# Solve operations of a hybrid decoder layer tied behind the large products, and a longer key chain

## The chip, the cores and the metric

One core of one Trainium2 chip runs the whole layer in one launch. The metric is device time in microseconds (us), the median of three runs.

## The reference

A decoder layer with two branches in parallel on 512 tokens of width 2048: sliding-window attention (32 query heads, 4 key heads of 64) and a gated delta rule (16 key heads, 32 value heads of 128, chunks of 64 tokens). Cut to what matters here:

```python
proj = h @ w_in                                    # all projections
d_qkv = causal_conv_silu(d_qkv, conv_w)
dk = jnp.repeat(l2_norm(dk), rep, axis=2)          # key norm
decay = jnp.exp(jnp.where(tril, g[..., :, None] - g[..., None, :], -jnp.inf))
L = jnp.where(strict, einsum('bhncd,bhnsd->bhncs', k_beta, k) * decay, 0.0)
t_inv = triangular_solve(eye + L, eye, lower=True, unit_diagonal=True)   # 64 x 64 per head and chunk
u = t_inv @ v_beta
w = t_inv @ (k_beta * jnp.exp(g)[..., None])
# then a scan over chunks with the state S, a norm, a gate, and the output products
```

## The kernel before

**Channel tiles.** Nearly all of TensorE's (PE's) work is `channel_tile`: one 128-channel slice of a projection for all 512 tokens, 16 contraction tiles, each as three products of split operands (`mm3`: L240 whi·hh, L241 whi·hl, L242 wlo·hh). So a tile is 48 large matmuls of 128x512. The weights come by DMA from SyncE's (SP's) queue into `raw` and are split into `whi` (ScalarE, ACT, L61) and `wlo` (VectorE, DVE, L62) half a tile at a time.

**Steps.** All other work is written as Python generators beside the tiles. After every second contraction tile (six large matmuls) `channel_tile` calls `pump()`, one step: generators in `live` count down the number that they yielded and continue at zero. The solve is in `slow`: it adds a budget of 0.36 a step and continues when it has saved up the number that it yielded. This is the order in which the program is written; a scheduler then lists each engine's instructions by this priority and by when its own model thinks that operands are ready, so an instruction written late can be issued early on an engine that the model sees idle. At run time each engine works through its list in order.

**Key stage** (`delta_keys`, about 155 to 545 us). Sixteen key heads g. For each: a channel tile, `conv` (ACT and DVE), a transpose `ptk` on PE (four matmuls), `sumsq` on ACT (junk, L686), `ss` and eleven small DVE operations on 128x4 for 1/sqrt (`rsqrt`: rky, rkt, L68 to L73), the scaled `k` on ACT (L653), its transpose `ptkT` on PE, `kT` (ACT), the Gram matrix `pkk` on PE (L668) and its product with the decay matrix E on DVE (L671), which DMA stores in `lt_d` and `lab_d`. E comes as a DMA broadcast of a row of `g_rows` (`decay_load`, L691), is masked on GpSimd (POOL, `decay_mask`, L698 and L699) and goes through exp on ACT (L663). Four buffers hold E, two for each head. Heads 4 to 7 follow each other tile by tile; from head 8 on a merge gate's tile (`mb`) stands between two keys. `ptk`, `ptkT` and `pkk` share two PSUM buffers.

**Solve** (`solve`, twice: b = 0 for the heads of keys 0 to 7, b = 1 for 8 to 15). When the keys are done, A (128 x 64 x 64) is loaded from `lt_d`, multiplied by -beta (L722), and inverted on DVE by 62 rounds, each a product into `atmp` (L729) and a sum into A (L735) of up to 992 elements. Then ACT copies four pieces to `ta_d` (L740), A is multiplied by beta (L745) and stored in `ts_d`. The second solve uses the same buffer.

**Attention** (`attention`, to about 1112 us): eight tiles for each of four groups n, beside them for each group the norm scales (`ssb`, `pss`), scores S, softmax (sm), their transposes pP copied to pT, and the product O. **Heads** (`delta_heads`, to about 2224 us): five tiles for each of 16 groups, beside them the query, value and gate chains and the scan (pp, r, pv, vn, vs, pd, S, po), with PE, DVE and ACT in turn. Groups 0 to 7 need the first solve, 8 to 15 the second. The output products follow.

Of the kernel before, what the change touches and what calls it, by code (L numbers as in the profile page):

```python
# [11 lines left out]
ALU = mybir.AluOpType  # L12
# [4 lines left out]
P = 128  # L17
# [8 lines left out]
HD = 64  # L26
# [19 lines left out]
class Layer:  # L46
# [190 lines left out]
    def mm3(self, ps, w, x, first, last):  # L237
        nc = self.nc
        (wh, wl), (xh, xl) = w, x
        nc.tensor.matmul(ps, lhsT=wh, rhs=xh, start=first, stop=False)  # L240
        nc.tensor.matmul(ps, lhsT=wh, rhs=xl, start=False, stop=False)  # L241
        nc.tensor.matmul(ps, lhsT=wl, rhs=xh, start=False, stop=last)  # L242

    def channel_tile(self, name, xh=None, xl=None):

# [391 lines left out]
    def keys(self, wk, g, ps):  # L637

        nc = self.nc
        y = wk.tile([P, T], F32, tag="y", name="y", bufs=3)  # L640
        yield from self.conv(wk, ps, 16 + g, y)
        E = [self.decay_load(wk, 2 * g + e) for e in range(2)]
        yield 2
        pt = self.ptp.tile([P, T], F32, tag="tp", name="ptk")
        self.transpose4(pt, lambda c: y[:, c * P : (c + 1) * P])
        ss = self.sumsq(wk, pt)
        yield 3
        nc.vector.tensor_scalar(out=ss, in0=ss, scalar1=EPS, scalar2=None, op0=ALU.add)
        rk = self.rsqrt(wk, ss, NTB, "rk")
        yield 2  # L650
        k = wk.tile([P, NTB, P], F32, tag="k", name="k")
        for c in range(NTB):
            nc.scalar.activation(k[:, c, :], pt[:, c * P : (c + 1) * P], AF.Copy, scale=rk[:, c : c + 1])  # L653
        for e in range(2):
            self.decay_mask(E[e], 2 * g + e)
        yield 3
        pt = self.ptp.tile([P, T], F32, tag="tp", name="ptkT")
        self.transpose4(pt, lambda c: k[:, c, :])
        nc.sync.dma_start(out=self.k_d[g], in_=k.rearrange("p c d -> p (c d)"))
        kT = wk.tile([P, T], F32, tag="kT", name="kT")  # L660
        nc.scalar.copy(out=kT, in_=pt)
        for e in range(2):
            nc.scalar.activation(E[e], E[e], AF.Exp)  # L663
        yield 2
        pk = self.ptp.tile([P, NTB, P], F32, tag="tp", name="pkk")
        for c in range(NTB):
            sl = slice(c * P, (c + 1) * P)
            nc.tensor.matmul(pk[:, c, :], lhsT=kT[:, sl], rhs=kT[:, sl], start=True, stop=True)  # L668
        nc.sync.dma_start(out=self.kT_d[g], in_=kT)
        for e in range(2):  # L670
            nc.vector.tensor_tensor(out=E[e], in0=pk, in1=E[e], op=ALU.mult)  # L671
        yield 2
        for e in range(2):
            h = 2 * g + e
            b, hl = h // 16, h % 16
            for k2 in range(2):
                s = slice(k2 * HD, (k2 + 1) * HD)
                nc.sync.dma_start(out=self.lt_d[b, k2, hl].rearrange("c j i -> j c i"), in_=E[e][s, :, s])
            nc.sync.dma_start(out=self.lab_d[h], in_=E[e][0:HD, :, HD:P])
        self.keys_done.append(g)  # L680
# [8 lines left out]
    def decay_load(self, wk, h):  # L689
        E = wk.tile([P, NTB, P], F32, tag="E", name="E", bufs=4)  # L690
        self.nc.sync.dma_start(out=E.rearrange("p c i -> p (c i)"), in_=self.g_rows[h].partition_broadcast(P))  # L691
        return E
# [10 lines left out]
    def solve(self, wk, b, eng):  # L703

        nc = self.nc
        while not all(g in self.keys_done for g in range(8 * b, 8 * b + 8)):
            yield 1.0
        A = wk.tile([P, HD, HD], F32, tag="A", name="A", bufs=1)
        bet = wk.tile([P, HD], F32, tag="bet", name="bet", bufs=1)
        for k2 in range(2):  # L710
            s = slice(k2 * HD, (k2 + 1) * HD)
            nc.sync.dma_start(
                out=A[s].rearrange("u j i -> u (j i)"), in_=self.lt_d[b, k2].rearrange("h c j i -> (h c) (j i)")
            )
            nc.sync.dma_start(
                out=bet[s],
                in_=self.b_rows.rearrange("h (c k i) -> k (h c) i", c=4, k=2)[k2, b * HD : (b + 1) * HD, :],
            )
        yield 8.0
        nb = wk.tile([P, HD], F32, tag="nbet", name="nbet", bufs=1)  # L720
        eng.tensor_scalar(out=nb, in0=bet, scalar1=-1.0, scalar2=None, op0=ALU.mult)
        eng.tensor_tensor(out=A, in0=A, in1=nb.unsqueeze(1).to_broadcast([P, HD, HD]), op=ALU.mult)  # L722
        eng.memset(A.rearrange("u j i -> u (j i)")[:, 0 : HD * HD : HD + 1], 1.0)
        for m in range(1, HD - 1):
            n = HD - 1 - m
            yield 0.2 + 0.0023 * m * n
            tmp = wk.tile([P, 1024], F32, tag="atmp", name="atmp", bufs=1)
            t = tmp[:, : m * n].rearrange("p (j i) -> p j i", j=m)
            eng.tensor_tensor(  # L729
                out=t,  # L730
                in0=A[:, m : m + 1, m + 1 :].to_broadcast([P, m, n]),
                in1=A[:, :m, m : m + 1].to_broadcast([P, m, n]),
                op=ALU.mult,
            )
            eng.tensor_tensor(out=A[:, :m, m + 1 :], in0=A[:, :m, m + 1 :], in1=t, op=ALU.add)  # L735
        for q in range(4):
            yield 1.5
            tmp = wk.tile([P, 1024], F32, tag="atmp", name="atmp", bufs=1)
            t = tmp.rearrange("p (i j) -> p i j", j=HD)[:HD]
            nc.scalar.copy(out=t, in_=A[:HD, :, q * 16 : (q + 1) * 16].rearrange("u j i -> u i j"))  # L740
            nc.sync.dma_start(
                out=self.ta_d[b].rearrange("h c i j -> (h c) (i j)")[:, q * 1024 : (q + 1) * 1024], in_=tmp[:HD]
            )
        yield 4.5
        eng.tensor_tensor(out=A, in0=A, in1=bet.unsqueeze(2).to_broadcast([P, HD, HD]), op=ALU.mult)  # L745
        for k2 in range(2):
            s = slice(k2 * HD, (k2 + 1) * HD)
            nc.sync.dma_start(
                out=self.ts_d[b, k2].rearrange("h c j i -> (h c) (j i)"), in_=A[s].rearrange("u j i -> u (j i)")
            )  # L750
# [765 lines left out]
```

## Time and profile before

| | |
|---|---|
| three runs | 2980.03, 2968.28, 2978.56 us; median 2978.56 |
| profiled execution | 2967.88 us, span 2966.1 us, mean granted clock 0.991 |
| busy, share of span | PE 97%, PEld 79%, DVE 60%, ACT 37%, POOL 7% |
| solve's rounds on DVE | L729: 124 operations, mean 883 ns; L735: 124, mean 894 ns; from 316.7 to 794.4 us |
| A times beta or -beta on DVE | L722 and L745: four operations of 4.42 us |
| solve's copies on ACT | L740: eight, median 2078 ns |

A stretch of a row of busy times gives each engine's busy us with the number of its instructions, then the share of full speed that PE's clock was granted, the DMA engines' busy share and GB/s. In rows in order of time the first number is the start, the second the duration, and the brackets give the idle time of that engine ahead of it and what ended it. Matmuls overlap, so their recorded durations (0.39 us for a large one) do not add up to a span.

### The profile page before, as it was taken

How to read it: one execution, taken by the hardware profiler on the slowest of the kernel's cores; microseconds unless marked ns; L12 is line 12 of the kernel's file. 1: busy time of each engine (PE TensorE's matmuls, PEld its weight loads, DVE VectorE, ACT ScalarE, POOL GpSimd, SP SyncE). 2: the span in 40 equal slices, each digit the busy share in tenths (PEclk: the TensorE clock that was granted, in tenths of full speed). 3: DMA queues.
4: the chain of work that ended last, by engine and by line, in shares of the span. 5: the costliest groups of instructions: out<-in, count | busy, mean ns of one | idle time of the engine just before them, and what ended most of it. 6: DMA issues, size and time to landing. Idle time of an engine off the chain costs nothing.

```text
span 2966.1 us, 38006 instructions
## 1 busy us (share of the span) xinstructions
PE 2876.7 (97%) x14524; PEld 2355.9 (79%) x14524; DVE 1775.4 (60%) x2903; ACT 1089.9 (37%) x2103; POOL 201.8 (7%) x188
## 2 busy tenths in 40 slices
PE   6899999999999999999999999999999999999999
PEld 5677777877878778888888888888887887888887
DVE  5766899699865544545454444454545555434666
ACT  3355333333543433333333333333333232222343
POOL 0012220010000000001100000000100000000000
PEclk8999999999999999999999999999999999999999
DMA  9855645632332233333333333334338998855684
GB/s 334 315 161 188 180 134 163 171 96 75 103 116 88 89 132 124 116 122 127 115 124 125 108 122 108 122 115 125 105 114 304 317 320 293 296 169 176 233 325 173
DMA packets 184871, 498.31 MB, mean 168 GB/s; under 512 B 75217, under 2 KB 77777, under 8 KB 147313
## 3 DMA queue, kind: packets, MB, share of 16 engines
q1 hardware_dynamic: 184690, 495.90, 50.1%
q8 instruction: 114, 1.87, 0.3%
q14 instruction: 67, 0.55, 0.1%
HBM read 415.26 MB, written 78.33 MB: 166 GB/s over the span
## 4 chain that ended last, share of the span: by engine, by line
PE 78%; DVE 11%; DMA 6%; ACT 2%; issue 2%; SPq 0%; POOL 0%; DVEq 0%; POOLq 0%; ACTq 0%
PE mm L240 21%; PE mm L241 20%; PE mm L242 20%; DVE wlo L62 2%; PE m L242 2%; PE m L241 2%; PE m L240 2%; DMA oraw<-o_d 2%; DVE A L735 2%; DVE atmp L729 2%; DVE wa L403 1%; DMA E<-g_rows 1%; DMA gw<-in_w_ada_gate 1%; PE po L901 1%; PE pv L882 1%
## 5 line engine op out<-in xcount | busy, mean ns | idle before, releaser
L240 PE MATMUL mm<-hh,whi 128*128 128x512 f32 x2784 | 1134.4, 407 | 3.6 <-ACT mth L263 3.6
L242 PE MATMUL mm<-hh,wlo 128*128 128x512 f32 x2784 | 1093.3, 393 | 0.0
L241 PE MATMUL mm<-hl,whi 128*128 128x512 f32 x2784 | 1091.0, 392 | 0.0
L62 DVE TENSOR_TENSOR wlo<-raw,whi 128x1024 fp32r<-128x1024 f32 (+1 forms) x484 | 590.2, 1221 | 483.7 <-ACT whi L61 460.5
L61 ACT CAST whi<-raw 128x1024 fp32r<-128x1024 f32 (+1 forms) x484 | 504.8, 1044 | 938.6 <-PE mm L241 829.9
L242 PEld LDWEIGHTS mm<-hh,wlo 128*128 128x128 f32 x2784 | 524.8, 189 | 114.2 <-issue 0.7
L240 PEld LDWEIGHTS mm<-hh,whi 128*128 128x128 f32 x2784 | 525.9, 189 | 112.5 <-issue 8.3
L241 PEld LDWEIGHTS mm<-hl,whi 128*128 128x128 f32 x2784 | 526.4, 189 | 99.6 <-issue 0.8
L240 PE MATMUL mm<-oh,whi 128*128 128x512 f32 x512 | 202.5, 397 | 6.9 <-ACT oh L61 6.9
L241 PE MATMUL mm<-ol,whi 128*128 128x512 f32 x512 | 201.6, 394 | 0.6 <-DVE ol L62 0.6
L242 PE MATMUL mm<-oh,wlo 128*128 128x512 f32 x512 | 201.0, 393 | 0.0
L240 PEld LDWEIGHTS mm<-oh,whi 128*128 128x128 f32 x512 | 97.0, 190 | 29.5 <-ACT oh L61 8.6
L241 PEld LDWEIGHTS mm<-ol,whi 128*128 128x128 f32 x512 | 97.2, 190 | 23.0 <-DVE ol L62 2.1
L242 PEld LDWEIGHTS mm<-oh,wlo 128*128 128x128 f32 x512 | 97.3, 190 | 20.4
L735 DVE TENSOR_TENSOR A<-A,atmp 128x62 f32<-128x62 f32 (+30 forms) x124 | 110.8, 894 | 2.0
L729 DVE TENSOR_TENSOR atmp<-A 128x62 f32<-128x62 f32 (+30 forms) x124 | 109.5, 883 | 1.6
L829 POOL TENSOR_TENSOR qe<-qe,yq 128x512 f32<-128x512 f32 x32 | 46.7, 1479 | 921.9 <-DMA qe<-eg_rows 921.9
L698 POOL TENSOR_TENSOR E<-E,neg_g 128x512 f32<-128x512 f32 x64 | 75.0, 1173 | 412.2 <-DMA E<-g_rows 356.9
L875 DVE SCALAR_TENSOR_TENSOR r<-pp,neg_eg,vt 128x128 f32<-128x128 f32 x96 | 29.3, 346 | 92.4 <-PE pp L872 90.5
L1220 ACT ACTIVATE sm<-sm,mx,rs 128x256 f32<-128x256 f32 (+1 forms) x128 | 71.8, 562 | 5.0 <-DVE mx L1215 5.0
L566 DVE SCALAR_TENSOR_TENSOR yv<-mm,convh,yv 128x511 f32<-128x511 f32 (+2 forms) x96 | 71.4, 744 | 1.7
L403 DVE SCALAR_TENSOR_TENSOR wa<-wa,silu_cb 128x2048 f32<-128x2048 f32 x24 | 54.8, 2283 | 6.5 <-DMA silu_cb<-silu_d 6.5
(337 smaller groups left out, 3025.9 us busy)
## 6 DMA issues: line engine op xcount, KB each, us to landing
raw<-in_w_ch SPq DMA_DIRECT2D x158, 1024.0 KB
wa<-in_w_ada_ss SPq DMA_DIRECT2D x32, 1024.0 KB
raw<-in_w_od SPq DMA_DIRECT2D x32, 1024.0 KB
E<-g_rows SPq DMA_DIRECT2D x64, 256.0 KB
q<-in_w_out SPq DMA_DIRECT2D x32, 512.0 KB
gw<-in_w_ada_gate SPq DMA_DIRECT2D x16, 1024.0 KB
f_d<-q SPq DMA_DIRECT2D x32, 512.0 KB
raw<-in_w_os SPq DMA_DIRECT2D x16, 1024.0 KB
```

What stands on the lines that cost most here:

```text
L61: self.nc.scalar.copy(out=hi, in_=src)
L62: self.nc.vector.tensor_tensor(out=lo, in0=src, in1=hi.bitcast(F32), op=ALU.subtract)
L240: nc.tensor.matmul(ps, lhsT=wh, rhs=xh, start=first, stop=False)
L241: nc.tensor.matmul(ps, lhsT=wh, rhs=xl, start=False, stop=False)
L242: nc.tensor.matmul(ps, lhsT=wl, rhs=xh, start=False, stop=last)
L403: nc.vector.scalar_tensor_tensor(out=wa, in0=wa, scalar=1.0, in1=scb, op0=ALU.mult, op1=ALU.mult, accum_out=t[:, j : j + 1])
L566: nc.vector.scalar_tensor_tensor(out=y[:, s:], in0=ps[:, : T - s], scalar=w[:, j : j + 1], in1=y[:, s:], op0=ALU.mult, op1=ALU.add)
L698: nc.gpsimd.tensor_tensor(out=E, in0=E, in1=ng, op=ALU.add)
L729: eng.tensor_tensor(out=t, in0=A[:, m : m + 1, m + 1 :].to_broadcast([P, m, n]), in1=A[:, :m, m : m + 1].to_broadcast([P, m, n]), op=ALU.mult,
L735: eng.tensor_tensor(out=A[:, :m, m + 1 :], in0=A[:, :m, m + 1 :], in1=t, op=ALU.add)
L829: nc.gpsimd.tensor_tensor(out=qf, in0=qf, in1=q, op=ALU.mult)
L1220: nc.scalar.activation(t, t, AF.Exp, scale=r[:, h : h + 1], bias=mx[:, h : h + 1], accum_out=den[:, h : h + 1])
```

## The change

Four edits, all in the order of work; no instruction is added or taken away.

1. `mm3` remembers its last matmul, and `behind` gives an instruction an edge for the scheduler: it is listed after that matmul. The edge carries no semaphore. All DVE operations of the solve but the memset get it, so each is listed after the large product that was written last before it.
2. Each solve round, one step of product and sum before, is two steps of half the length, with the sum in the second.
3. In the key chain the pause between 1/sqrt and k goes from 2 steps to 4, and that between k and ptkT from 3 to 4. ptkT is written 3+4+4 = 11 steps (66 large matmuls) behind ptk, where it was 3+2+3 = 8 (48).
4. The two loads of decay rows move from two steps ahead of ptk to three steps behind it.

```diff
+        self.last_mm = nc.tensor.matmul(ps, lhsT=wl, rhs=xh, start=False, stop=last)
+    def behind(self, ins):
+        self.tc.add_manual_dep(
+            ins.ins, self.last_mm.ins.name, mybir.DependencyInfo(mybir.DependencyClass.NoSync, mybir.DependencyReason.DATA),
+            reason="pace",
+        )
...
         yield from self.conv(wk, ps, 16 + g, y)
-        E = [self.decay_load(wk, 2 * g + e) for e in range(2)]
         yield 2
         pt = self.ptp.tile([P, T], F32, tag="tp", name="ptk")
...
         yield 3
+        E = [self.decay_load(wk, 2 * g + e) for e in range(2)]
         nc.vector.tensor_scalar(out=ss, in0=ss, scalar1=EPS, scalar2=None, op0=ALU.add)
         rk = self.rsqrt(wk, ss, NTB, "rk")
-        yield 2
+        yield 4
...
             self.decay_mask(E[e], 2 * g + e)
-        yield 3
+        yield 4
...
         for m in range(1, HD - 1):
             n = HD - 1 - m
-            yield 0.2 + 0.0023 * m * n
+            yield 0.1 + 0.00115 * m * n
...
-            eng.tensor_tensor(
...
+            self.behind(
+                eng.tensor_tensor(
...
-            eng.tensor_tensor(out=A[:, :m, m + 1 :], in0=A[:, :m, m + 1 :], in1=t, op=ALU.add)
+            yield 0.1 + 0.00115 * m * n
+            self.behind(eng.tensor_tensor(out=A[:, :m, m + 1 :], in0=A[:, :m, m + 1 :], in1=t, op=ALU.add))
```

The edges reach the multiplications of A by -beta and by beta in the same way.

The order that results is compared at three places, all on DVE. Lines of the changed kernel are 7 to 10 higher (L648 is L655, L729 and L735 of the solve are L737 and L745, L722 is L729). First, key chain 13 in the key stage, from ss on; A and atmp are the solve's, rky and rkt the chain's. Before:

```order
L648 TENSOR_SCALAR ss<-ss 128x4
L735 TENSOR_TENSOR A<-A,atmp 128x33x30
L68 TENSOR_SCALAR rky<-ss 128x4
L62 TENSOR_TENSOR wlo<-raw,whi 128x1024
L71 SCALAR_TENSOR_TENSOR rkt<-rky 128x4
L729 TENSOR_TENSOR atmp<-A 128x986
L72 TENSOR_TENSOR rkt<-rkt,ss 128x4
L735 TENSOR_TENSOR A<-A,atmp 128x34x29
L73 SCALAR_TENSOR_TENSOR rky<-rkt,rky 128x4
L729 TENSOR_TENSOR atmp<-A 128x980
L71 SCALAR_TENSOR_TENSOR rkt<-rky 128x4
L62 TENSOR_TENSOR wlo<-raw,whi 128x1024
```

Now:

```order
L655 TENSOR_SCALAR ss<-ss 128x4
L68 TENSOR_SCALAR rky<-ss 128x4
L71 SCALAR_TENSOR_TENSOR rkt<-rky 128x4
L72 TENSOR_TENSOR rkt<-rkt,ss 128x4
L73 SCALAR_TENSOR_TENSOR rky<-rkt,rky 128x4
L71 SCALAR_TENSOR_TENSOR rkt<-rky 128x4
L62 TENSOR_TENSOR wlo<-raw,whi 128x1024
L72 TENSOR_TENSOR rkt<-rkt,ss 128x4
L73 SCALAR_TENSOR_TENSOR rky<-rkt,rky 128x4
L737 TENSOR_TENSOR atmp<-A 128x752
L71 SCALAR_TENSOR_TENSOR rkt<-rky 128x4
L72 TENSOR_TENSOR rkt<-rkt,ss 128x4
```

Between ss and the chain's last rky stood eight solve operations and two wlo; now one of each stands there. The solve has also come less far (752 elements on the way up, where it was at 986 on the way down).

Second, attention, where the changed kernel has the second solve's first multiplication (A by -beta, L729) and the softmax's copies pT of group 2; the kernel before has no solve operation between the two copies there.

```order
L1238 TENSOR_SCALAR sm<-sm,den 128x256 x8
L62 TENSOR_TENSOR wlo<-raw,whi 128x1024 x2
L728 TENSOR_SCALAR nbet<-bet 128x64
L1250 COPY pT<-pP 128x512
L729 TENSOR_TENSOR A<-A,nbet 128x4096
L1064 TENSOR_TENSOR partner_4384<-partner_4384,sin 128x512
L730 MEMSET A 128x64
L1065 TENSOR_TENSOR aq<-aq,partner_4384 128x512
L737 TENSOR_TENSOR atmp<-A 128x62
L1250 COPY pT<-pP 128x512
```

The multiplication of 4096 elements and one round's product now stand ahead of the second copy.

Third, the heads, in the tiles of group 2, where the scan's S and r stand between the query's convolution (yq). Before:

```order
L912 SCALAR_TENSOR_TENSOR S<-S,egl,pd 128x128 x2
L62 TENSOR_TENSOR wlo<-raw,whi 128x1024
L566 SCALAR_TENSOR_TENSOR yq<-mm,convh,yq 128x511
L566 SCALAR_TENSOR_TENSOR yq<-mm,convh,yq 128x510
L566 SCALAR_TENSOR_TENSOR yq<-mm,convh,yq 128x509
L875 SCALAR_TENSOR_TENSOR r<-pp,neg_eg,vt 128x128 x2
L573 SCALAR_TENSOR_TENSOR yq<-th,yq 128x512
L62 TENSOR_TENSOR wlo<-raw,whi 128x1024
```

Now:

```order
L922 SCALAR_TENSOR_TENSOR S<-S,egl,pd 128x128 x2
L62 TENSOR_TENSOR wlo<-raw,whi 128x1024
L573 SCALAR_TENSOR_TENSOR yq<-mm,convh,yq 128x511
L737 TENSOR_TENSOR atmp<-A 128x950
L573 SCALAR_TENSOR_TENSOR yq<-mm,convh,yq 128x510
L885 SCALAR_TENSOR_TENSOR r<-pp,neg_eg,vt 128x128 x2
L573 SCALAR_TENSOR_TENSOR yq<-mm,convh,yq 128x509
L580 SCALAR_TENSOR_TENSOR yq<-th,yq 128x512
L745 TENSOR_TENSOR A<-A,atmp 128x38x25
L62 TENSOR_TENSOR wlo<-raw,whi 128x1024
```

A product of the second solve has come between the convolution's parts ahead of r, and its sum behind them. In the whole head stage 74 such operations have come, the last of them in group 5; before there were none. On PE only ptkT and pkk, and some of the attention's pP and O, stand at another point between the large products.

More of the change, by code (lines that the diff above doesn't have):

```diff
@@ L241, in mm3 @@
         nc.tensor.matmul(ps, lhsT=wh, rhs=xl, start=False, stop=False)
-        nc.tensor.matmul(ps, lhsT=wl, rhs=xh, start=False, stop=last)
+        self.last_mm = nc.tensor.matmul(ps, lhsT=wl, rhs=xh, start=False, stop=last)
[4 more added lines that the diff above has]
+        )
     def channel_tile(self, name, xh=None, xl=None):
@@ L720, in solve @@
         nb = wk.tile([P, HD], F32, tag="nbet", name="nbet", bufs=1)
-        eng.tensor_scalar(out=nb, in0=bet, scalar1=-1.0, scalar2=None, op0=ALU.mult)
-        eng.tensor_tensor(out=A, in0=A, in1=nb.unsqueeze(1).to_broadcast([P, HD, HD]), op=ALU.mult)
+        self.behind(eng.tensor_scalar(out=nb, in0=bet, scalar1=-1.0, scalar2=None, op0=ALU.mult))
+        self.behind(eng.tensor_tensor(out=A, in0=A, in1=nb.unsqueeze(1).to_broadcast([P, HD, HD]), op=ALU.mult))
         eng.memset(A.rearrange("u j i -> u (j i)")[:, 0 : HD * HD : HD + 1], 1.0)
@@ L725, in solve @@
             n = HD - 1 - m
-            yield 0.2 + 0.0023 * m * n
+            yield 0.1 + 0.00115 * m * n
             tmp = wk.tile([P, 1024], F32, tag="atmp", name="atmp", bufs=1)
             t = tmp[:, : m * n].rearrange("p (j i) -> p j i", j=m)
[L729 to L733, printed above, removed]
-            )
-            eng.tensor_tensor(out=A[:, :m, m + 1 :], in0=A[:, :m, m + 1 :], in1=t, op=ALU.add)
+            self.behind(
+                eng.tensor_tensor(
+                    out=t,
+                    in0=A[:, m : m + 1, m + 1 :].to_broadcast([P, m, n]),
+                    in1=A[:, :m, m : m + 1].to_broadcast([P, m, n]),
+                    op=ALU.mult,
+                )
+            )
+            yield 0.1 + 0.00115 * m * n
+            self.behind(eng.tensor_tensor(out=A[:, :m, m + 1 :], in0=A[:, :m, m + 1 :], in1=t, op=ALU.add))
         for q in range(4):
@@ L744, in solve @@
         yield 4.5
-        eng.tensor_tensor(out=A, in0=A, in1=bet.unsqueeze(2).to_broadcast([P, HD, HD]), op=ALU.mult)
+        self.behind(eng.tensor_tensor(out=A, in0=A, in1=bet.unsqueeze(2).to_broadcast([P, HD, HD]), op=ALU.mult))
         for k2 in range(2):
```

## Prediction

> **What bounds the kernel now.** I read the page first, then busy time in stretches cut at the borders of the channel tiles, then the order of time around the gaps on TensorE (PE).
>
> ```profile
> span 2966.1 us, 38006 instructions
> PE 2876.7 (97%) x14524; PEld 2355.9 (79%) x14524; DVE 1775.4 (60%) x2903; ACT 1089.9 (37%) x2103; POOL 201.8 (7%) x188
> ```
>
> PE is busy for 97% of the span: the kernel ends when PE has issued its products. An edit to VectorE's (DVE's) order can gain only where PE waits for DVE, at most some 90 us. The next view has one row for each pair of channel tiles in the key stage: width, busy time of PE, PEld, DVE, ACT, POOL, granted clock, DMA share, GB/s. Each pair holds 96 large products and about one key chain.
>
> ```profile
> 257.47:288.15 30.68, 27.05 (x129) 22.47 (x128) 17.20 (x38) 14.20 (x36) 8.59 (x10) 0.94 0.59 182
> 288.15:312.70 24.55, 24.55 (x121) 20.60 (x120) 12.65 (x24) 10.62 (x26) 2.09 (x3) 1.00 0.77 211
> 312.70:340.51 27.81, 25.92 (x113) 20.88 (x112) 26.12 (x45) 9.95 (x23) 5.37 (x5) 0.94 0.61 191
> 340.51:370.85 30.34, 25.45 (x113) 20.78 (x112) 28.73 (x39) 11.41 (x25) 11.47 (x9) 0.94 0.44 144
> 370.85:398.52 27.67, 25.55 (x113) 20.80 (x112) 25.77 (x36) 9.94 (x23) 4.32 (x4) 0.94 0.35 110
> 398.52:426.36 27.84, 25.22 (x113) 20.58 (x113) 26.00 (x34) 10.05 (x23) 6.23 (x4) 0.94 0.43 139
> 426.36:454.18 27.82, 25.32 (x113) 20.67 (x113) 26.36 (x35) 10.04 (x23) 6.33 (x4) 0.94 0.45 145
> 454.18:479.97 25.79, 23.96 (x113) 19.56 (x113) 25.59 (x36) 10.07 (x23) 7.11 (x6) 1.00 0.45 143
> ```
>
> The pair at 288.15 runs undisturbed: 24.55 us, PE never idle, clock 1.00. From 312.70 on DVE is busy for 26 to 29 us of each pair, more than PE needs for one: in this stage DVE is the bound. The difference is the solve, whose instructions alone are these (DVE, ACT, then clock and DMA):
>
> ```profile
> 288.15:312.70 24.55, 0.62 (x1) 0.00 (x0) 1.00 0.77 211
> 426.36:454.18 27.82, 15.22 (x14) 0.00 (x0) 0.94 0.45 145
> ```
>
> How this reaches PE, for key chain 13 (DVE, ACT and PE rows in order of time):
>
> ```profile
> 426.90 0.16 DVE L648 TENSOR_SCALAR ss<-ss 128x4 f32<-128x4 f32 x1
> 432.94 1.01 DVE L71 SCALAR_TENSOR_TENSOR rkt<-rky 128x4 f32<-128x4 f32 x1
> 437.53 1.16 DVE L729 TENSOR_TENSOR atmp<-A 128x972 f32<-128x972 f32 x1
> 439.12 0.39 PE L242 MATMUL mm<-hh,wlo 128*128 128x512 f32 x1
> 441.39 0.15 DVE L73 SCALAR_TENSOR_TENSOR rky<-rkt,rky 128x4 f32<-128x4 f32 x1
> 441.58 1.15 ACT L653 ACTIVATE k<-ptk,rky 128x128 f32<-128x128 f32 x4 [0.21 <-DVE rky L73]
> 442.00 0.47 PE L274 MATMUL ptkT<-ident,k 128*128 128x128 f32 x1 [2.50 <-ACT k L653]
> 442.13 0.77 PE L240 MATMUL mm<-hh,whi 128*128 128x512 f32 x1
> ```
>
> Eleven small operations on 128x4, 0.15 us each when nothing disturbs them, take from 426.90 to 441.54, since solve operations stand between them. ACT scales k only then, and PE, in order, stands at ptkT for 2.50 us. The large product behind it takes 0.77 instead of 0.39 us: the clock has dropped.
>
> **The change, part by part.** It is summed against the profiled execution's own time, 2967.88 us (span 2966.1).
>
> *Key stage.* PE's idle time is width minus busy: 3.63, 0, 1.89, 4.89, 2.12, 2.62, 2.50 and 1.83, together 19.5 us. Six of the rows have clock 0.94; their widths sum to 172.2 us, and 6% of it is 10.3 us. So 29.8 us can be had here.
>
> With the edges, six solve operations stand between one chain's ss and the next one's, where there were 12 to 14; at 15.22/14 = 1.09 us each that takes DVE from 26.4 to about 26.4 - 15.2 + 6.5 = 17.7 us in a pair that needs 24.55. In chain 13 itself, one solve operation and one wlo (1.2 us) remain between ss and the last rky, where there were eight and two: at 1.1 to 1.2 us each some 9.4 us fewer, against the 2.50 us that PE waited. Three more steps between ss and ptkT add room: a step is 24.55/16 = 1.53 us, so 4.6 us for chains whose ptkT stood 48 large products behind ptk and now stands 66 behind; chains 11 to 14 stood at 62 to 67 already and gain by the shorter DVE queue. I leave 3 us, between 0 and 12 (three stalls like the one at 426.36: 2.50 + 1.7 each), for the chain that now meets the 4.42 us multiplication of A at its head. Gain 27.
>
> *Decay rows five steps later.* The stall in the row at 257.47 came before any solve operation. Its chain:
>
> ```profile
> 263.53 1.05 POOL L698 TENSOR_TENSOR E<-E,neg_g 128x512 f32<-128x512 f32 x1 [4.67 <-DMA E<-g_rows]
> 264.65 1.57 POOL L699 TENSOR_SCALAR_AFFINE_SELECT E<-E 128x512 f32<-128x512 f32 x1
> 266.26 0.63 ACT L663 ACTIVATE E<-E 128x512 f32<-128x512 f32 x1 [4.70 <-POOL E L699]
> 271.30 1.14 ACT L653 ACTIVATE k<-ptk,rky 128x128 f32<-128x128 f32 x4 [2.95 <-DVE rky L73]
> 257.71 5.69 DMA E<-g_rows
> 367.74 4.89 DMA E<-g_rows
> ```
>
> ACT stood 4.70 us for the mask on POOL, which waited for the rows, and with ACT the th that DVE's queue needed. The last two rows, from the chain of waits, give 4.9 to 5.7 us from a load's issue to its use. The load now comes three steps behind ptk and its product E with pkk 13 steps behind ptk; ten steps are 15.3 us, and 5.7 for the load, 2 x (1.05 + 1.57) on POOL and 2 x 0.63 on ACT make 12.2. It fits with 3.1 us to spare, and the loads ask for their buffers later, so SP stands less for the stores of chain g-2. Cost nothing, cover 3.1 us; if it is gone, the E exponentials hold ACT and kT is late next. The gain on this stall is in the 27.
>
> *Attention.* The four groups do equal work; each row is half a group:
>
> ```profile
> 615.37:671.32 55.95, 51.49 (x269) 40.86 (x269) 54.70 (x85) 17.06 (x34) 2.02 (x1) 0.97 0.26 80
> 671.32:729.67 58.35, 54.83 (x281) 42.77 (x281) 58.11 (x87) 23.47 (x52) 5.55 (x3) 1.00 0.21 73
> 729.67:789.24 59.57, 59.46 (x373) 47.16 (x373) 58.31 (x114) 24.18 (x55) 1.28 (x1) 1.00 0.29 98
> 789.24:846.16 56.92, 54.41 (x289) 43.52 (x289) 41.88 (x75) 32.30 (x58) 4.06 (x3) 1.00 0.51 143
> 903.57:957.72 54.15, 54.15 (x289) 43.52 (x289) 35.44 (x65) 24.40 (x54) 3.94 (x3) 1.00 0.27 90
> 957.72:1015.12 57.40, 57.40 (x365) 45.84 (x365) 31.79 (x75) 22.96 (x53) 1.29 (x1) 1.00 0.26 86
> 625.89 0.91 PE L1170 MATMUL pss<-ident,ssb 128*128 128x128 f32 x4 [4.46 <-DVE ssb L1166]
> 817.16 4.42 DVE L745 TENSOR_TENSOR A<-A,bet 128x4096 f32<-128x4096 f32 x1 [2.72 <-ACT atmp L740]
> 822.24 1.75 PE L1247 MATMUL O<-pT,vtok_a 128*64 128x128 f32 x28 [2.50 <-DVE pT L1240]
> ```
>
> Against the last group, without a solve, the rows lose 58.35 - 54.15 = 4.20, 59.57 - 57.40 = 2.17 and 56.92 - 54.15 = 2.77 us; the row at 615.37 loses 4.46 idle and 3% of clock, 1.7. Together 15.3 us. The solves now run through all of attention at half that density. New: the 4.42 us product of A and -beta stands ahead of one of two pT copies, as the product with beta did at 817.16, where PE lost 2.5 us. I leave 5 of the 15.3 (one such stall with clock, 4.2, and crumbs); bounds 0 and 15.3. Gain 10.
>
> *Heads.* Seventy-four solve operations, all in the second solve, move into the first six head groups, some 75 us of DVE work. There DVE has room (first row), and the scan's r, ready at 1259.50, is used by pv at 1261.46:
>
> ```profile
> 1240.80:1644.64 403.84, 403.84 (x2138) 336.15 (x2137) 201.00 (x378) 150.68 (x337) 36.29 (x36) 1.00 0.37 119
> 1258.89 0.61 DVE L875 SCALAR_TENSOR_TENSOR r<-pp,neg_eg,vt 128x128 f32<-128x128 f32 x2
> 1261.46 0.60 PE L882 MATMUL pv<-r,tt 128*128 128x128 f32 x4
> ```
>
> The 1.96 us cover one operation of 1.2 us. The 4.42 us product with beta stands once ahead of the E product with pqk. I take 2 us of loss, between 0 and 10 (1.6 us in each of six groups). PE's written order is otherwise unchanged here.
>
> *The edges and the halved steps* add no instruction, and no wait on PE: in the built program the solve operations wait for DVE and DMA alone, as before. Cost nothing; nothing is queued behind a new wait.
>
> Sum: 27 + 10 - 2 = 35 us, 2967.88 - 35 = 2933. The profiled execution equals the lowest of the runs shown (2968.28); the others are 2978.56 and 2980.03. Two of four lie near 2968 and two near 2979, so I add half the distance, 5.5: **2938 us**.
>
> A rule to weigh: the six rows with clock 0.94 followed PE gaps of 1.89 to 4.89 us. The Trainium skill, "TensorE: Matmul & The Clock Gate", section "What's actually happening", lets the clock fall only after an idle window of about 3.4 us. By that rule only three of the gaps above (3.63, 4.89, 4.46) would have cost clock, and the gain would be 4 x 1.7 = 6.8 us smaller; the rows show the drop after 1.89 to 2.62 us too, so the trace disagrees and the sum stands by the rows.
>
> **Rivals.**
>
> *The heads give it back (slower).* If DVE has no slack at the scan's hand-overs, each solve operation there delays PE by its length. For it: r, vs, S and vn alternate between PE and DVE in every group. Against: 1.96 us of slack, and the attention row at 671.32, with DVE busy 58.11 of 58.35 us, lost only 4.20. In full it costs 75 us: 2967.9 - 37 + 75 = 3006. It decides from 37/75, half of the work exposed.
>
> *The edges don't touch what is late.* Then the late masks on POOL hold the chains, as at 263.53 without any solve, and loading later does not help: the key stage keeps its 29.8. Against: the undisturbed pair at 288.15 had the same masks. Only attention gains: 2967.9 - 10 + 5.5 = 2963.
>
> *Spread but not relieved.* The key stage gains its 27, attention none, as the solves stay in it longer, and the heads lose 5: 2967.9 - 22 + 5.5 = 2951.
>
> **How the numbers follow.** Forecast 0.70, spread 0.17, edges miss 0.09, heads 0.04. Low end: all of 29.8 + 15.3 from 2967.9, 2922. High end: between the second-best case and the third, 2960; about 0.13 is left above it. A measurement here tells 0.5% from no change, 14.9 us: faster means under 2963.7. All of the forecast and of the spread case are faster, 0.87; the 2963 case counts as same, 0.09; slower 0.04.
>
> **What would show it.** Right: rows of the key stage with PE idle under 1 us each and clock 1.00, DVE near 18 us a pair; solve operations from about 340 us to about 1500 us; head groups still 67 us. Wrong: ptkT waiting for k by over 2 us in more than two chains, pv or pu waiting for DVE in the first six groups, or ACT standing for POOL ahead of k.

## The result and the profile after

The changed kernel takes 2941.45 us (median of 4 runs, 2938.28 to 2947.28); beside it the kernel before took 2973.42 us (2966.49 to 2980.03). The ratio is 0.9894, 95% interval 0.9874 to 0.9915: faster by about 1.1%. The profiled execution took 2939.34 us.

```profile
span 2937.5 us, 37979 instructions
PE 2865.5 (98%) x14524; PEld 2350.7 (80%) x14524; DVE 1764.5 (60%) x2903; ACT 1088.3 (37%) x2103; POOL 208.6 (7%) x188
```

PE is still the bound; 28.6 us of span went, 11.2 of them out of its busy time, in which stretches of slower clock count in full. The pairs of key tiles, cut and laid out as in the prediction (width; busy PE, PEld, DVE, ACT, POOL; clock; DMA share; GB/s):

```profile
255.49:281.04 25.55, 25.55 (x130) 21.38 (x128) 17.35 (x38) 15.33 (x42) 8.15 (x8) 1.00 0.61 198
281.04:306.12 25.08, 25.08 (x126) 20.99 (x124) 12.26 (x23) 11.38 (x24) 6.75 (x6) 1.00 0.90 240
306.12:329.77 23.65, 23.65 (x113) 19.70 (x112) 14.02 (x23) 9.43 (x21) 1.69 (x2) 1.00 0.64 184
329.77:354.46 24.69, 23.91 (x114) 19.62 (x112) 20.16 (x39) 10.98 (x24) 9.20 (x8) 1.00 0.61 194
...
425.42:449.07 23.65, 23.65 (x113) 19.70 (x112) 16.34 (x27) 10.05 (x22) 5.33 (x5) 1.00 0.51 151
```

PE is idle in one of eight pairs (0.78 us), and the clock is whole. DVE has about 16 us of work in a pair of 23.65, where it had 26; only the pair with the solve's first, short rounds has 20. The solve alone in the last pair (DVE, ACT), and key chain 13:

```profile
425.42:449.07 23.65, 6.29 (x6) 0.00 (x0) 1.00 0.51 151
```

```profile
425.82 0.17 DVE L655 TENSOR_SCALAR ss<-ss 128x4 f32<-128x4 f32 x1 [0.18 <-ACT junk L693]
429.27 0.16 DVE L73 SCALAR_TENSOR_TENSOR rky<-rkt,rky 128x4 f32<-128x4 f32 x1
429.46 1.14 ACT L660 ACTIVATE k<-ptk,rky 128x128 f32<-128x128 f32 x4 [2.24 <-DVE rky L73]
439.05 0.60 PE L281 MATMUL ptkT<-ident,k 128*128 128x128 f32 x4
```

The chain takes 3.6 us instead of 14.6, and k lies ready 8.5 us before ptkT.

By stages, the kernel before first: key stage (from the second mb tile to the first key tile of attention), attention, and head groups 0 to 5.

```profile
166.42:547.33 380.91, 360.40 (x1669) 296.10 (x1668) 291.52 (x477) 164.59 (x356) 73.75 (x66) 0.97 0.54 169
570.99:1112.69 541.70, 528.94 (x2948) 422.53 (x2946) 404.36 (x721) 219.43 (x458) 31.21 (x26) 1.00 0.31 100
1112.69:1510.07 397.38, 397.38 (x2088) 330.29 (x2089) 192.17 (x349) 145.24 (x316) 37.64 (x36) 1.00 0.38 121
```

```profile
166.05:515.77 349.72, 348.88 (x1669) 289.73 (x1668) 223.41 (x408) 156.11 (x350) 69.30 (x66) 1.00 0.57 176
539.43:1069.19 529.76, 525.62 (x2948) 420.99 (x2946) 393.40 (x712) 218.32 (x458) 35.49 (x26) 1.00 0.34 106
1069.19:1484.77 415.58, 404.40 (x2089) 334.76 (x2089) 259.32 (x425) 152.30 (x320) 44.17 (x36) 0.98 0.40 124
```

So the key stage gained 31.2 us and attention 11.9, and the heads lost 18.2. The remaining 4 us lie in stages that the change doesn't touch (the start, and the wait for transfers behind the heads). The heads' loss, group by group (1 to 5):

```profile
1132.07:1202.21 70.14, 67.45 (x359) 55.95 (x358) 46.71 (x75) 25.02 (x57) 7.77 (x6) 1.00 0.35 114
1202.21:1273.86 71.65, 69.07 (x360) 57.22 (x358) 45.76 (x75) 25.02 (x57) 8.09 (x6) 0.98 0.35 111
1273.86:1345.75 71.89, 69.00 (x360) 57.18 (x358) 46.59 (x78) 25.03 (x57) 7.70 (x6) 0.98 0.35 111
1345.75:1417.46 71.71, 68.95 (x360) 57.14 (x358) 45.16 (x88) 28.85 (x59) 7.49 (x6) 0.98 0.38 116
1417.46:1484.77 67.31, 67.31 (x360) 56.03 (x358) 37.65 (x64) 28.94 (x59) 6.33 (x6) 1.00 0.57 160
```

An undisturbed group takes 67.3 us. Group 0 takes 62.88 us instead of 60.85. In groups 1 to 4 PE stands once, and the table of waits (engine, what it waited for, us in total, times, longest) says for what:

```profile
PE ptv L281 <- DVE yv L580: 10.9, 4, 2.9
```

ptv is the transpose of the first value tile. Group 2, in order of time on POOL, ACT, DVE and PE:

```profile
1232.09 3.90 POOL L839 TENSOR_TENSOR qe<-qe,yq 128x512 f32<-128x512 f32 x2 [61.80 <-DVE osb L941]
1235.96 1.94 POOL L705 TENSOR_TENSOR E<-E,neg_g 128x512 f32<-128x512 f32 x1
1239.69 0.63 POOL L706 TENSOR_SCALAR_AFFINE_SELECT E<-E 128x512 f32<-128x512 f32 x1
1238.64 0.63 ACT L833 ACTIVATE E<-E 128x512 f32<-128x512 f32 x1 [6.56 <-POOL E L706]
1240.36 0.63 ACT L833 ACTIVATE E<-E 128x512 f32<-128x512 f32 x1 [1.09 <-POOL E L706]
1240.90 1.03 ACT L61 CAST whi<-raw 128x1024 fp32r<-128x1024 f32 x1
1241.83 0.62 ACT L578 ACTIVATE th<-yv 128x512 f32<-128x512 f32 x1
1236.91 0.73 DVE L573 SCALAR_TENSOR_TENSOR yv<-mm,convh,yv 128x509 f32<-128x509 f32 x1
1242.49 0.69 DVE L580 SCALAR_TENSOR_TENSOR yv<-th,yv 128x512 f32<-128x512 f32 x1 [3.65 <-ACT th L578]
1243.33 1.02 PE L281 MATMUL ptv<-ident,yv 128*128 128x128 f32 x4 [2.58 <-DVE yv L580]
1244.00 0.78 PE L240 MATMUL mm<-hh,whi 128*128 128x512 f32 x1
```

DVE had yv summed at 1237.64; th, which needs nothing else, came 4.2 us later. In ACT's order, ahead of th stood two exponentials that waited for POOL's masks, and a whi cast. The large product behind ptv takes 0.78 us instead of 0.39: the clock is halved. In the kernel before, th stood between the two exponentials:

```profile
1275.68 0.63 ACT L823 ACTIVATE E<-E 128x512 f32<-128x512 f32 x1 [4.97 <-POOL E L699]
1276.22 0.61 ACT L571 ACTIVATE th<-yv 128x512 f32<-128x512 f32 x1
1277.40 0.63 ACT L823 ACTIVATE E<-E 128x512 f32<-128x512 f32 x1 [0.57 <-POOL E L699]
```

So the order on ACT that the scheduler wrote is this, before and after:

```
L823 ACTIVATE E<-E 128x512
L571 ACTIVATE th<-yv 128x512
L823 ACTIVATE E<-E 128x512
L61 CAST whi<-raw 128x1024
```

```
L833 ACTIVATE E<-E 128x512 x2
L61 CAST whi<-raw 128x1024
L578 ACTIVATE th<-yv 128x512
```

The likely reason is the scheduler's own model: with solve operations in DVE's queue it expects yv later, and lists what it expects to be ready earlier, the exponentials and the cast, ahead of th. No run shows the model itself, but the order goes with the solve: from group 5 on, where the rounds have ended, the old order is back, and it stands from group 1 on in the two kernels below whose groups 1 to 4 hold no rounds (without the second solve's rounds, and at pace 0.5).

### The profile page after: what moved, and what is told of

Its sections match the earlier page's. It is cut to its first block, busy times and chain, and to the rows that moved or that the text cites. A ratio compares the mean times of both kernels' runs of the same rounds, so it can differ in the third digit from the quotient of the medians.

```text
span 2937.5 us, 37979 instructions
## 1 busy us (share of the span) xinstructions
PE 2865.5 (98%) x14524; PEld 2350.7 (80%) x14524; DVE 1764.5 (60%) x2903; ACT 1088.3 (37%) x2103; POOL 208.6 (7%) x188
## 4 chain that ended last, share of the span: by engine, by line
PE 85%; DMA 6%; DVE 4%; ACT 2%; issue 1%; POOL 1%; SPq 0%; POOLq 0%; DVEq 0%; ACTq 0%
PE mm L240 23%; PE mm L242 22%; PE mm L241 22%; DMA gw<-in_w_ada_gate 2%; PE m L242 2%; PE m L240 2%; PE m L241 2%; DMA oraw<-o_d 2%; DVE wa L410 1%; PE S L1206 1%; PE pv L892 1%; PE po L911 1%; PE O L1257 1%; PE pP L281 1%; PE po L910 1%
## 5 line engine op out<-in xcount | busy, mean ns | idle before, releaser
L62 DVE TENSOR_TENSOR wlo<-raw,whi 128x1024 fp32r<-128x1024 f32 (+1 forms) x484 | 596.4, 1233 | 490.8 <-ACT whi L61 473.4
L745 DVE TENSOR_TENSOR A<-A,atmp 128x62 f32<-128x62 f32 (+30 forms) x124 | 111.1, 896 | 0.6
L737 DVE TENSOR_TENSOR atmp<-A 128x62 f32<-128x62 f32 (+30 forms) x124 | 109.3, 882 | 0.6
L1230 ACT ACTIVATE sm<-sm,mx,rs 128x256 f32<-128x256 f32 (+1 forms) x128 | 71.7, 562 | 3.8 <-DVE mx L1225 3.8
L1433 DVE SCALAR_TENSOR_TENSOR gate_bc<-gw,silu_c,gate_bc 128x2048 f32<-128x2048 f32 x15 | 35.2, 2350 | 42.1 <-DMA gw<-in_w_ada_gate 42.1
```

The source lines that it names most:

```text
L62: self.nc.vector.tensor_tensor(out=lo, in0=src, in1=hi.bitcast(F32), op=ALU.subtract)
L737: eng.tensor_tensor(out=t, in0=A[:, m : m + 1, m + 1 :].to_broadcast([P, m, n]), in1=A[:, :m, m : m + 1].to_broadcast([P, m, n]), op=ALU.mult,
L745: self.behind(eng.tensor_tensor(out=A[:, :m, m + 1 :], in0=A[:, :m, m + 1 :], in1=t, op=ALU.add))
L1230: nc.scalar.activation(t, t, AF.Exp, scale=r[:, h : h + 1], bias=mx[:, h : h + 1], accum_out=den[:, h : h + 1])
L1433: nc.vector.scalar_tensor_tensor(out=acc, in0=w, scalar=s, in1=acc, op0=ALU.mult, op1=ALU.add)
```

## The experiments

Times are medians of 4 to 6 runs; ratios are to the kernel before, which ran beside them (2972.7 to 2973.1 us).

**What carries the key stage.** First the edges without the longer key chain:

```
         yield from self.conv(wk, ps, 16 + g, y)
+        E = [self.decay_load(wk, 2 * g + e) for e in range(2)]
...
-        E = [self.decay_load(wk, 2 * g + e) for e in range(2)]
...
-        yield 4
+        yield 2
         k = wk.tile([P, NTB, P], F32, tag="k", name="k")
...
-        yield 4
+        yield 3
         pt = self.ptp.tile([P, T], F32, tag="tp", name="ptkT")
```

> The edges and the halved steps alone; the key chain and its decay loads stand as before the change. Theory (the edges carry the gain): the key stage keeps most of its 31 us, since solve operations stand 5 to 7 to a pair of tiles either way; only the later room between ss and ptkT is missing, which was 4.6 us per chain against stalls of 2.5 us: 2941 to 2949. Rival (the longer key chain carries it): PE stands for ptkT and pkk as before the change, the key stage keeps its 29.8 us of loss and only attention gains: 2958 to 2968.

2952.46 us, ratio 0.9933 (0.9917 to 0.9948). Then the reverse, the longer chain and later loads without edges and halved steps:

```
-            self.behind(eng.tensor_tensor(...))
+            eng.tensor_tensor(...)
-            yield 0.1 + 0.00115 * m * n    (twice in a round)
+            yield 0.2 + 0.0023 * m * n     (once)
```

> The longer key chain and the later decay loads alone; no edges, no halved steps. Theory (the edges carry it): DVE still has 13 solve operations in a pair of key tiles, 26 us of work where PE needs 24.55, so PE must lose 1.5 to 2 us a pair wherever the chain stands, attention is as before, heads undisturbed: 2955 to 2970. Rival (the chain's room carries it): the key stage gains its 30 us without any edge, the heads lose nothing: 2938 to 2948, as fast as the whole change or faster.

2951.87 us, 0.9927 (0.9910 to 0.9943). Neither theory holds by itself: each half gains 21 us, both 32. The key stage takes 358.5 us with the edges, 365.6 with the chain, 349.7 with both. The rows say which half works where: the edges' kernel first, in the pair ahead of any solve operation and in one with it; then the chain's, twice with the solve.

```profile
260.80:291.22 30.42, 27.65 (x129) 22.61 (x128) 16.60 (x39) 14.17 (x37) 8.72 (x9) 0.94 0.55 178
315.83:339.49 23.66, 23.66 (x114) 19.70 (x112) 16.78 (x25) 10.15 (x22) 5.63 (x5) 1.00 0.67 218
```

```profile
328.93:357.19 28.26, 25.78 (x114) 20.98 (x112) 27.12 (x41) 11.08 (x24) 11.81 (x8) 0.94 0.45 152
411.18:438.78 27.60, 25.41 (x113) 20.75 (x112) 26.04 (x34) 10.05 (x22) 6.59 (x4) 0.94 0.42 138
```

Without the longer chain the early pair is as bad as before (30.42); there is no solve for the edges to move. Without the edges DVE has 26 us in a pair that PE does in 23.65, and three more steps mend only part of that: the six pairs with the solve take 159.2 us, where they took 167.3 before and take 143.0 with both. Attention gains by the edges alone (530.1 against 540.8 us).

The decay loads at their old place, all else changed:

```
         yield from self.conv(wk, ps, 16 + g, y)
+        E = [self.decay_load(wk, 2 * g + e) for e in range(2)]
...
-        E = [self.decay_load(wk, 2 * g + e) for e in range(2)]
```

> The whole change, but the decay rows are loaded at their old place, behind the convolution of k. Theory (the load's place is worth nothing): within 3 us of the changed kernel, 2938 to 2945, and the pair of tiles at 257 us is as short as with the later load. Rival (the later load took away the 4.7 us wait of ACT for the masks in that pair): that stall of 3.6 us idle and 1.7 us of clock is back, 2945 to 2950.

2943.09 us, 0.9900 (0.9883 to 0.9916); key stage 348.4 us, and the first of the pairs 25.5. With the three steps in place, the load's place is worth nothing that can be measured. Later loads without the steps were not run.

The rounds of the solve not halved:

```
-            yield 0.1 + 0.00115 * m * n    (ahead of each operation)
+            yield 0.2 + 0.0023 * m * n     (once, ahead of both)
```

> The whole change without the halved steps: each round's product and sum are issued together behind one large product, a round's whole step apart. Theory (the edges spread the solve, halving only splits a pair): pairs of operations of 2.3 us stand together where a hand-over can hide 1 to 3 us; within 4 us of the changed kernel, 2938 to 2945. Rival (the halving matters: two operations together hold k's chain and the scan's r for twice as long): stalls of 1 to 2 us come back in the key stage and in the heads, 2946 to 2956.

2941.20 us, 0.9894 (0.9877 to 0.9911): halving is worth nothing that can be measured.

**What the heads pay for.** The second solve without its rounds; its loads, its products of all of A and its stores stay:

```
-        for m in range(1, HD - 1):
+        for m in range(1, HD - 1) if b == 0 else ():
```

> The whole change, with the 62 rounds of the second solve left out (its loads, its two products of all of A and its stores stay), so DVE has no solve operations from the middle of attention on. Theory (solve operations in the head groups make yv late, and PE stands for ptv): the four gaps of 2.7 to 3.1 us ahead of ptv in groups 1 to 4 are gone with their half clock, 16 us, and 2 to 4 us of attention: 2919 to 2925. Rival (yv is late because ACT has th behind the two E exponentials that POOL holds up, whatever DVE does): the four gaps stay, 2935 to 2941.

2925.29 us, 0.9841 (0.9822 to 0.9860), 0.3 us above the theory's range: the heads gave what it said, but the 2 to 4 us in attention did not come (529.9 us). Head groups 0 to 5:

```profile
1068.36:1467.31 398.95, 398.95 (x2089) 331.41 (x2089) 192.85 (x349) 145.25 (x316) 37.63 (x36) 1.00 0.38 121
```

PE is never idle. In this kernel the scheduler has th between the exponentials again, so it does not tell DVE's work from ACT's order. The next two do: one edge from th of the first value tile to the second exponential, then to both. The solve stays; by the traces the orders of DVE, POOL and PE are those of the changed kernel, instruction by instruction.

```
+        self.last_th = nc.scalar.activation(th, y, AF.Tanh)
...
+            ins = nc.scalar.activation(M[e], M[e], AF.Exp)
+        self.tc.add_manual_dep(ins.ins, self.last_th.ins.name, ...NoSync..., reason="order")
```

> The whole change and one more issue-order edge on ACT alone: in each head group the second E exponential is issued behind the th of the first value tile. The orders of DVE, POOL and PE stay as they are, the 31 or so solve operations of the first four groups too. Theory (yv is late because ACT's order in groups 1 to 4 puts th behind both E exponentials and so behind both masks of POOL): th moves up by one mask and one exponential, from 1241.83 to about 1240.2 in group 2, ptv's gap shrinks from 2.6 us to about 1, short enough to leave the clock whole: 3 to 3.5 us in each of four groups, 2926 to 2931. Rival (DVE's solve operations slow POOL and stand ahead of yv on DVE, whatever ACT's order): the gaps stay over 2 us with their half clock, 2936 to 2942.

2927.70 us, 0.9852 (0.9833 to 0.9870). The gaps shrank to 0.87 to 1.19 us, with whole clock. (Groups 1 to 4 hold 64 solve operations by the trace, not 31.) Group 2:

```profile
1235.49 0.63 ACT L578 ACTIVATE th<-yv 128x512 f32<-128x512 f32 x1
1236.02 0.61 ACT L833 ACTIVATE E<-E 128x512 f32<-128x512 f32 x1
1236.98 0.63 PE L281 MATMUL ptv<-ident,yv 128*128 128x128 f32 x4 [0.87 <-DVE yv L580]
```

Both exponentials behind th (the edge inside the loop over e):

> As the kernel with the edge on the second exponential, with the same edge on the first too: th of the first value tile ahead of both E exponentials in every head group, DVE's and POOL's orders unchanged. Theory (th waits for POOL only through ACT's order): th goes as soon as DVE has summed yv, the gaps of 1.0 to 1.3 us that were left ahead of ptv in groups 1 to 4 are gone, 4 to 5 us under the kernel with one edge: 2921 to 2926. Rival (the exponentials, up to 0.6 us later, make E late for the products of the scan, in all 16 groups): groups from 5 on grow from 67.3 us, 2928 to 2940.

**2925.96 us, 0.9835 (0.9813 to 0.9858): 15 us under the change by the medians.** Against the kernel with one edge 4 to 5 us were expected; the medians differ by 1.7, within the intervals, and the head groups by 3.3 us. Gaps of 1.00 and 0.73 us are left in groups 3 and 4. Its heads:

```profile
1067.29:1466.77 399.48, 397.75 (x2088) 330.07 (x2089) 265.67 (x425) 152.06 (x320) 49.69 (x37) 1.00 0.42 129
```

DVE has 266 us of work in these groups against 192 before the change, and PE loses 2.1 us by it. So the solve's work costs 2 us in the heads, and ACT's order cost the other 16. Groups from 5 on stay at 67.3 us, against the rival.

**A longer wait instead of the order.** ptv two steps later:

```
         yield from self.conv(wk, ps, 32 + 2 * g + e, y)
-        yield 2
+        yield 4
```

> The whole change, with ptv two steps (3.06 us) further behind yv in each value tile. Theory: the four gaps of 2.7 to 3.1 us ahead of ptv are covered, the scan behind it starts two steps later and has room: 16 us less in groups 1 to 4, 2923 to 2929. Rival (the wait moves on to the scan: vt comes later for r and pv): the 16 us come back there in part, 2932 to 2942.

3008.27 us, 1.0120 (1.0101 to 1.0140): both theories missed. From group 1 on every head group takes 72 to 74 us, to the end of the stage, those without a solve too. ptv is covered, but pto, the transpose of the scan's output, now stands:

```profile
1603.59 0.15 DVE L934 SCALAR_TENSOR_TENSOR ms<-osq,epsq 128x4 f32<-128x4 f32 x1
1604.38 0.91 DVE L68 TENSOR_SCALAR roy<-ms 128x8 int32<-128x8 int32 x1
1605.85 0.98 DVE L71 SCALAR_TENSOR_TENSOR rot<-roy 128x8 f32<-128x8 f32 x1
1606.87 0.97 DVE L72 TENSOR_TENSOR rot<-rot,ms 128x8 f32<-128x8 f32 x1
1607.88 0.17 DVE L73 SCALAR_TENSOR_TENSOR roy<-rot,roy 128x8 f32<-128x8 f32 x1
1612.08 1.11 PE L281 MATMUL pto<-ident,osb 128*128 128x128 f32 x4 [3.88 <-DVE osb L941]
```

The new order on DVE puts the norm chain of the output (roy, rot) among the convolution's operations and beside POOL's qe and masks (1603.97 to 1610.67). There four of the 128x8 operations take 0.91 to 0.98 us instead of 0.17.

**Another pace.** Both solves at 0.5 in place of 0.36, so that they end ahead of the heads:

```
-            self.solves = self.paced(self.solve_all(), 0.36)
+            self.solves = self.paced(self.solve_all(), 0.5)
```

> The whole change with the solves paced at 0.5 in place of 0.36 per step, so that both end ahead of the first head group. Theory: heads undisturbed as before the change (60.9 and 67.3 us a group), 18 us gained; attention has 7 to 12 solve operations in a pair of tiles where the change left 4 to 7 and before had 14, and gives back 2 to 5 us: 2924 to 2930. Rival (attention's half groups lose again what they lost before the change, 4.2, 2.2 and 2.8 us each, now for both solves): 2933 to 2945.

2932.54 us, 0.9867 (0.9850 to 0.9884). Neither range holds it. The heads do nearly as the theory says (400.7 us), but attention gives back 10 us (539.9), not 2 to 5. Then 0.40, with th first:

> The same with the solves paced at 0.40 in place of 0.36 per step: the second solve ends some 30 us earlier in the heads. Theory (with ACT's order mended the heads no longer pay for the solve, so its pace is worth nothing there, and attention holds up to 8 operations in a pair of tiles without loss but for one heavier pair): within 4 us of the kernel at 0.36, 2921 to 2929. Rival (attention pays, as at 0.5): 2929 to 2935.

2933.37 us, 0.9859 (0.9838 to 0.9881): the number is the rival's, the reason is not. Of the 8.4 us that attention lost, 8.3 are one pair of tiles (41.5 us instead of 33.2). Its rows, and the matching ones at pace 0.5:

```profile
819.32 4.41 DVE L729 TENSOR_TENSOR A<-A,nbet 128x4096 f32<-128x4096 f32 x1
824.25 1.22 DVE L62 TENSOR_TENSOR wlo<-raw,whi 128x1024 fp32r<-128x1024 f32 x1
825.53 0.79 PE L242 MATMUL mm<-hh,wlo 128*128 128x512 f32 x1 [4.12 <-DVE wlo L62]
```

```profile
702.92 4.43 DVE L729 TENSOR_TENSOR A<-A,nbet 128x4096 f32<-128x4096 f32 x1
709.97 0.46 PE L1206 MATMUL S<-kd,aq 64*128 64x128 f32 x2 [1.86 <-DVE rqy L73]
```

At 0.40 it is the one product of all of A that heads the second solve, landing ahead of a split that PE needs. At 0.5 the same product stands ahead of rqy, for which PE waits 1.86 us, and the clock is halved for 6.8 us from 711.5 on; that makes about 5 of the 10 us, and where the rest went was not traced. To test the reading at 0.40, the same kernel with the product in four parts:

```
-        self.behind(eng.tensor_tensor(out=A, in0=A, in1=nb...[P, HD, HD], op=ALU.mult))
+        for q in range(4):
+            r = slice(q * 16, (q + 1) * 16)
+            self.behind(eng.tensor_tensor(out=A[:, r], in0=A[:, r], in1=nb...[P, 16, HD], op=ALU.mult))
+            yield 1.2
```

> As the kernel paced at 0.40, with the product of A and -beta at the head of each solve cut into four of 128x1024, a step and more apart. Theory (what the pace of 0.40 lost, 8.2 us in one pair of attention tiles, is the single 4.41 us operation ahead of a wlo split): no gap over 2 us is left in attention, 2922 to 2927, level with the kernel at 0.36 that has th first. Rival (it is the denser solve that loses in attention): 2929 to 2936 as before the cut.

2927.19 us, 0.9850 (0.9833 to 0.9866). Attention takes 527.5 us, the pair 33.2: the loss has left the pair with that operation. The four parts do not stand where the whole stood, though. With the pauses between them they run from 839.3 to 855.0 us, 20 us and more later, in tiles that lose nothing either. Whether the shorter operations or the other place did it, this run does not tell. In the heads one gap of 2.16 us with half clock came up in group 4, so the whole is level with the version at 0.36, not better.

## Why the prediction came out as it did

The forecast was 2938 us, the range 2922 to 2960; 2941.45 came. That it lies within 4 us is luck: the heads took 16 us more than forecast, and four smaller misses the other way made up for most of it.

**Key stage, 27 predicted, 31.2 measured.** Mechanism and size were right: six solve operations in the last pair (predicted six), DVE at about 16 us there (17.7). Of the 29.8 us counted in the eight pairs 28.9 came (222.5 to 193.6), the rest from just outside them. The 3 us kept for the chain behind the product of A and -beta were not needed; one gap of 0.8 us is all. What the prediction didn't separate, the two single halves did: the edges do most for the chains with a solve, the three steps do all for those ahead of it.

**Decay rows later, nothing predicted, nothing measured** (the run with early loads). The stall at 257 us, told there by the late rows, is covered by the chain's room: with early loads and three more steps it is gone, and with early loads and no more steps it is back.

**Attention, 10 predicted, 11.9 measured.** The 5 us left for the product of A and -beta were not spent: at 880.36 it ran for 4.92 us ahead of the second pT copy (886.73), as was said, but PE did not stand for it (26.00 us busy from 874 to 900). That was luck of place; at the pace 0.40 it cost 8 us. The 11.9 already hold a loss of 1.7 us in the last tile ahead of the heads (15.0 us, before 13.3). There ACT's order is that of before, and the masks that its exponentials wait for come later; with th first the tile takes 12.6.

**Heads, 2 predicted, bounds 0 to 10, 18.2 measured: the term that was mis-sized.** The step that failed reads: "The 1.96 us cover one operation of 1.2 us", with bounds of 1.6 us a group. It measured the slack where DVE hands r to PE, and that hand-over held. The loss came at yv, th, ptv: four gaps of 2.58 to 2.89 us and the clock behind three of them, 16 us in all. There the slack depended on ACT's place for th, and that order the change rewrote though its diff names neither ACT nor th. The prediction compared the orders of DVE and said that PE's was otherwise unchanged; it did not look at ACT's. Its sign for being right, head groups still at 67 us, failed (70 to 72), and none of its signs for being wrong named ptv. The row before (th at 1276.22, between two exponentials that wait for POOL) showed how little room there was.

**Edges and halved steps, nothing.** Halving: right. The edges themselves: no wait was added, as said, but by moving DVE's work they changed the order that the scheduler writes on ACT, most likely through its own time for yv.

**Sum.** 27 + 10 - 2 was to be 35; it was 31.2 + 11.9 - 18.2 = 24.9, plus 4 us elsewhere, mostly transfers that vary from run to run: 28.5 between the two profiled executions. The forecast also held 5.5 us for slower executions; the median lies 2.1 us above the profiled one.

**The rivals.** *The heads give it back* was put down to DVE's work standing at hand-overs; the kernel with th first carries all that work for 2.1 us, so that mechanism is refuted, while its sign showed through another. *The edges don't touch what is late* holds for the chains ahead of the first solve operation alone. *Spread but not relieved* did not occur in attention, which gained; its loss in the heads came, but 18 us instead of 5 and by ACT's order.

## What to carry to other kernels

Where a scheduler writes the orders, moving work on one engine can rewrite another's queue: compare all engines' orders around each hand-over, above all behind instructions that wait on a slow engine. An edge between two instructions of the late engine can then be worth more than moving the work again or adding steps; two more steps ahead of ptv cost 67 us over the change. A single long operation is priced by what stands behind it in its queue: the same 4.4 to 4.9 us cost nothing in one place and 8 us in another.

## What the runs showed of the hardware

VectorE and GpSimd hold each other up in these rows. With solve operations beside it POOL's first mask addition took 1.94 us instead of 1.05 and two qe products 3.90, against 2.61 in the kernel before and 3.04 in the one without the second solve's rounds; DVE's wlo took 1.66 us instead of 1.22. It looks like waiting rather than a common slowing. In the kernel with ptv later the six slow operations among the 128x8 ones each end within 0.04 us of the end of a POOL instruction: those that start at 1604.38, 1605.85 and 1606.87 end at 1605.29, 1606.83 and 1607.84, and POOL's two qe products and first mask addition at 1605.26, 1606.81 and 1607.82. The Trainium skill, "GPSIMD Engine Reference", section "8. Key points", says that the two share their interfaces to memory, and that they contend where a DVE instruction has two inputs from it or runs in a 2-port mode. The rows agree for wlo and the solve's sums, which have two inputs; the TENSOR_SCALAR roy (0.91 us) has one, and whether it ran in such a mode no run here shows.

Whether a gap on PE costs clock is not set by its length alone. In the changed kernel the gaps of 2.58, 2.89 and 2.76 us ahead of ptv each cost 1.6 to 1.8 us more than themselves (the groups take 71.7 to 71.9 us instead of 67.3), and the one of 2.69 us in group 1 only 0.1 (70.1 us). The granted clock is 0.50 for 3.41 us beside each of the three, which is 1.7 us of work, and 1.00 beside the fourth. In the kernel with the longer chain alone a gap of 1.84 us lay in a pair with clock 0.94, and one of 2.10 us in a pair with 1.00. No single gap under 1.84 us cost clock in the key stage, attention and the heads of any run here. To shorten the gap in group 2 from 2.58 to 0.87 us was so worth 3.3 us (71.65 to 68.36), not 1.7.

The time of the same stage differs between executions: three output tiles that wait for transfers (at about 2423 us) took 39.6 us in the changed kernel, 43.4 before, and 46.6 and 46.8 in two others that don't touch them (the edges alone, and th between).
